# Attention scores in row groups of 64 queries and two heads over 192 keys, instead of 128 queries of one head over 256

## The chip, the cores and the metric

The kernel runs on one core of one Trainium2 chip. The metric is the device time of one launch in microseconds (us): 1665.48 us, the median of three runs (1665.45 to 1665.97). TensorE (PE) multiplies matrices, VectorE (DVE) and ScalarE (ACT) work elementwise, GpSimd (POOL) does small copies, clears and part of the DMA issues, SyncE (SP) issues the other DMAs. PEld is TensorE's weight load, which runs beside its matmuls. Each engine works through its own instructions in a fixed order and waits for the others at semaphores.

## The reference, cut to what matters

One layer of a hybrid decoder, in f32, for two request groups with shared weights: 1024 prompt tokens and 8 sample sequences of 8 tokens each (64 tokens), which makes T = 1088 columns. One input projection gives q (16 heads of 64), k and v (4 heads of 64), the two halves of a gated unit and two gates. Branch A is attention with a window of 128 and one learned sink per head:

```python
delta = i + WINDOW - j                       # query i of a block of 128, key j of 256: the block before and this one
band = (delta >= 0) & (delta < WINDOW)
s = einsum('bnqkgd,bnskd->bnkgqs', q, k) * HEAD_DIM ** -0.5
s = where(mask, s, NEG_INF)
p = softmax(concatenate([s, sink], -1))[..., :-1]
o = einsum('bnkgqs,bnskd->bnqkgd', p, v)
```

A query i can see only the keys i < j <= i + 128 of the 256. The sample tokens see their 128 cached keys and the new keys of their own sequence. Branch B is a gated unit, a causal depthwise convolution of width 31, LayerNorm, swish and a projection. Both branches are gated and added, and an output projection, a feed-forward part with a convolution of width 3, and the norms follow.

## The kernel before

**Numbers.** Most products are computed in three f32r matmuls of split operands (high by high, high by low, low by high; `mm3`, L190 to L192), for each of eight k tiles of 128 rows. Tokens go in three chunks of 384, 384 and 320 columns.

**Stages.** Weight tiles stream in an order that is written out by hand (`SEQUENCE`): q, k, v, the gated unit's halves b and a, and the gates. When k and v of a half are there, the attention of half p = 0 (heads 0 to 7) and later of p = 1 runs between the k tiles of the other streams. After that come the output product of the attention (`phase_y`, which reloads half 0 of the attention output from DRAM, L935 and L936), LayerNorm, the output projection, the feed-forward part, and the tail.

**The attention units.** `plan_units(p)` makes a list of steps for eight blocks of 128 queries and four sample units, each with a due time counted in k tiles. `tick()` is called at each k tile and issues the steps that are due. A block has two halves g. For each half there is one `scores` step (due 0 and 5), `turn` steps (due 14 and 19; one each for the keys of the block before and of this one) and a `mix` step (due 20 and 25). Blocks follow each other after 22 k tiles in half 0 and 19 in half 1.

- `scores`: four heads, each two matmuls (L396, L397) with 128 queries of one head as the weights and 256 keys as columns (128 keys in block 0), into PSUM banks "aux".
- `softmax`: GpSimd copies the four sinks into the fifth column group of the tile p (L362). VectorE scales, masks and takes the row minimum in one operation for each head (L368, the reduce). ScalarE takes exponentials with the sum (L373), VectorE the reciprocal (L375), ScalarE normalises (L377).
- `turn`: four transposes (L406), then the result is split into a high part by ScalarE (L225, pth) and a low part by VectorE (L226, ptl).
- `mix`: products with v (L418, L419), copied and added into the tile av (L424, L425). At the second half the result is split back into the q tiles, which so become the attention's output. Half 0 is written to DRAM by GpSimd (`attn_spill`, L443, L444).
- `sample_unit`: two f32 matmuls against the cached keys kp and two against the new keys ks (L459), a softmax with one reduce for each of the two, two transposes and the mix.

**The convolution of branch B** (`conv`) runs on VectorE alone, as 44 multiply-adds of 512 or 513 columns (L520) for each of eight channel tiles. Nothing in the attention reads it. Its place in VectorE's order is not written out: it is issued with a lower priority,

```python
with self.later(CONV_LATER):   # CONV_LATER = 1200: this many instructions later in the order of priorities
    self.conv(i, u)
```

and the scheduler that builds the kernel puts each of its operations, by its own estimate of times, where VectorE has nothing of higher priority that is ready. The order so found is fixed in the built kernel.

**Layouts.** q is a tile of [128, 4, 1088]: two heads of 64 dimensions on the partitions (one half g live, the other the low part), four head pairs, the tokens. `masks` holds 640 columns: the band of 256, the cached keys' 128, four times 64 new keys. The tile p is [128, 4, 260], a new one for each `scores` step out of two buffers.

Of the kernel before, what the change touches and what calls it, by code (L numbers as in the profile page):

```python
# [6 lines left out]
F32 = mybir.dt.float32  # L7
# [110 lines left out]
MTOT = 2 * WIN + WIN + 4 * NS  # L118


class Build:
# [237 lines left out]
    def softmax(self, parts, pt, lo, width, nsink):  # L359
        nc = self.nc  # L360
        n = len(parts)
        nc.gpsimd.tensor_copy(pt[:, :, width:width + 1], nsink[:, :, None])  # L362
        nm = self.t(self.at, [P, 4], "nm", bufs=4)
        den = self.t(self.at, [P, 4], "den", bufs=4)
        for j in range(n):
            least = nsink[:, j:j + 1]
            for o, s, mask in parts[j]:
                nc.vector.tensor_tensor_reduce(  # L368
                    out=pt[:, j, o:o + s.shape[1]], in0=s, in1=mask, scale=-(HD ** -0.5), scalar=least,
                    op0=ALU.add, op1=ALU.min, accum_out=nm[:, j:j + 1])  # L370
                least = nm[:, j:j + 1]
        for j in range(n):
            nc.scalar.activation(pt[:, j, lo:width + 1], pt[:, j, lo:width + 1], AF.Exp, bias=nm[:, j:j + 1],  # L373
                                 scale=-1.0, accum_out=den[:, j:j + 1])
        nc.vector.reciprocal(den[:, :n], den[:, :n])  # L375
        for j in range(n):
            nc.scalar.activation(pt[:, j, lo:width], pt[:, j, lo:width], AF.Identity, scale=den[:, j:j + 1])  # L377

    def attn_unit(self, p, blk, st):
        nc = self.nc  # L380
        q, kd, kl = st["q"], st["kd"], st["kl"]
        qs = slice(blk * P, (blk + 1) * P)
        lo = WIN if blk == 0 else 0
        keys = slice((blk - 1) * P + lo, (blk + 1) * P + lo)
        mask = self.masks[:, lo:2 * WIN]
# [3 lines left out]
        def scores(g):  # L389
            pt = live[g]["pt"] = self.t(self.at, [P, 4, 2 * WIN + 4], "p", bufs=2)  # L390
            s = []
            for jj in range(2):
                ps = self.bank("aux").rearrange("p (a b) -> p a b", a=2)
                for j in range(2):
                    h = 2 * jj + j
                    nc.tensor.matmul(ps[:, j, :], q[g][:, h, qs], kd[g][:, keys], start=True, stop=False)  # L396
                    nc.tensor.matmul(ps[:, j, :], q[g][:, h, qs], kl[g][:, keys], start=False, stop=True)  # L397
                    s.append([(lo, ps[:, j, :2 * WIN - lo], mask)])
            hd = 4 * (2 * p + g)
            self.softmax(s, pt, lo, 2 * WIN, self.nsink[:, hd:hd + 4])  # L400

        def turn(g, kb):
            pt = live[g]["pt"]
            ps = self.bank("aux")
            for h in range(4):
                nc.tensor.transpose(ps[:, h * P:(h + 1) * P], pt[:, h, kb * P:(kb + 1) * P], self.ident)  # L406
# [5 lines left out]
        def mix(g):  # L412
# [27 lines left out]
    def attn_spill(self, st, cols):  # L440
        nc = self.nc
        for j in range(4):
            nc.gpsimd.dma_start(self.d_ah[j, :, cols], st["q"][0][:, j, cols].bitcast(F32))  # L443
            nc.gpsimd.dma_start(self.d_al[j, :, cols], st["q"][1][:, j, cols].bitcast(F32))  # L444

    def sample_unit(self, p, bp, st):
# [4 lines left out]
        def scores():  # L451
            kp = self.t(self.at, [P, 2, WIN], "kp", bufs=1)
            vp = live["vp"] = self.t(self.at, [P, 2, P], "vp", bufs=1)
            nc.gpsimd.dma_start(kp, self.a["kpT"][p, :, 2 * bp:2 * bp + 2, :])
            nc.gpsimd.dma_start(vp, self.a["vp"][2 * bp:2 * bp + 2, :, p * P:(p + 1) * P].rearrange("b k d -> k b d"))
            ps = self.bank("aux")
            for d, x in ((slice(0, WIN), lambda b: kp[:, b, :]), (slice(WIN, 192), lambda b: k)):
                for b in range(2):
                    nc.tensor.matmul(ps[:, d], q[:, bp, b * HD:b * HD + P], x(b), start=b == 0, stop=b == 1)  # L459
# [14 lines left out]
        def mix():  # L474
# [7 lines left out]
            cs = slice(SEQ + 2 * bp * NT, SEQ + 2 * bp * NT + 2 * NT)  # L482
            for g in range(2):
                r = slice(g * HD, (g + 1) * HD)
                src = ov[r, g]
                dh = st["q"][0][r, :, cs].rearrange("p j (b t) -> p j b t", b=2)
                dl = st["q"][1][r, :, cs].rearrange("p j (b t) -> p j b t", b=2)
                self.split_ps(dh, dl, src)
            if p == 0 and bp == 3:
                self.attn_spill(st, slice(SEQ, T))  # L490
# [106 lines left out]
    def run(self):  # L597
        nc, tc, a = self.nc, self.tc, self.a
        es = ExitStack()
        with es:  # L600
            dp = es.enter_context(tc.tile_pool(name="dram", bufs=1, space=bass.MemoryType.DRAM))
            self.d_ah = self.t(dp, [4, P, T], "d_ah")
# [1075 lines left out]
```

## Time and profile before

| | |
|---|---|
| median of three runs | 1665.48 us (1665.45 to 1665.97) |
| span of the profiled execution | 1662.4 us |
| outside the span, against that median | 3.1 us |
| TensorE busy | 1652.5 us (99%) |
| VectorE busy | 1337.3 us (80%) |
| ScalarE busy | 866.3 us (52%) |
| GpSimd busy | 290.2 us (17%) |
| granted TensorE clock | nine tenths or more in every slice |

Rows of the profile name a line of the code, an engine, an operation and its tiles (out<-in). In a timeline the first number is the start and the second the duration, in microseconds from the start of the span. In a table of stretches the columns are named in its first line, and (x) is the number of instructions.

### The profile page before, as it was taken

How to read it: one execution, taken by the hardware profiler on the slowest of the kernel's cores; microseconds unless marked ns; L12 is line 12 of the kernel's file. 1: busy time of each engine (PE TensorE's matmuls, PEld its weight loads, DVE VectorE, ACT ScalarE, POOL GpSimd, SP SyncE). 2: the span in 40 equal slices, each digit the busy share in tenths (PEclk: the TensorE clock that was granted, in tenths of full speed). 3: DMA queues.
4: the chain of work that ended last, by engine and by line, in shares of the span. 5: the costliest groups of instructions: out<-in, count | busy, mean ns of one | idle time of the engine just before them, and what ended most of it. 6: DMA issues, size and time to landing. Idle time of an engine off the chain costs nothing.

```text
span 1662.4 us, 29877 instructions
## 1 busy us (share of the span) xinstructions
PE 1652.5 (99%) x11550; PEld 1636.9 (98%) x11550; DVE 1337.3 (80%) x2432; ACT 866.3 (52%) x1781; POOL 290.2 (17%) x483
## 2 busy tenths in 40 slices
PE   9999999999999999999999999999999999999998
PEld 9999999999999999999999999999999999999997
DVE  7899979999989986855545896777887786988867
ACT  6424368774488845973233454444444454524222
POOL 0100112231011111110000171344444320000000
PEclk9999999999999999999999999999999999999999
DMA  6221212232121265544343332244444324766403
GB/s 208 84 71 42 75 60 81 99 103 86 55 53 48 77 227 168 178 154 145 106 155 108 80 125 103 97 113 115 112 114 111 94 103 134 243 168 168 118 14 108
DMA packets 98623, 187.09 MB, mean 113 GB/s; under 512 B 22848, under 2 KB 57680, under 8 KB 98464
## 3 DMA queue, kind: packets, MB, share of 16 engines
q1 hardware_dynamic: 79152, 125.18, 24.3%
q0 software_dynamic: 18896, 59.72, 11.9%
q8 instruction: 91, 1.49, 0.4%
q14 instruction: 52, 0.43, 0.1%
q10 hardware_dynamic: 432, 0.27, 0.1%
HBM read 129.75 MB, written 57.35 MB: 113 GB/s over the span
## 4 chain that ended last, share of the span: by engine, by line
PE 91%; DVE 5%; ACT 2%; DMA 1%; issue 1%; ACTq 0%; DVEq 0%; SPq 0%
PE mm L190 23%; PE mm L192 23%; PE mm L191 23%; PE aux L190 6%; PE aux L192 6%; PE aux L191 6%; PE aux L406 1%; DVE c L520 1%; PE aux L418 1%; PE aux L419 1%; PE aux L396 1%; PE aux L397 1%; DVE bt L520 1%; DVE q L739 1%; DMA bw<-d_b 0%
## 5 line engine op out<-in xcount | busy, mean ns | idle before, releaser
L190 PE MATMUL mm<-xh,whi 128*128 128x384 f32 (+1 forms) x904 | 301.1, 333 | 0.0
L191 PE MATMUL mm<-xl,whi 128*128 128x384 f32 (+1 forms) x904 | 295.4, 327 | 0.1
L192 PE MATMUL mm<-xh,wlo 128*128 128x384 f32 (+1 forms) x904 | 295.4, 327 | 0.0
L191 PEld LDWEIGHTS mm<-xl,whi 128*128 128x128 f32 x904 | 170.0, 188 | 1.6 <-DVE xl L277 0.7
L190 PEld LDWEIGHTS mm<-xh,whi 128*128 128x128 f32 x904 | 169.8, 188 | 0.7
L192 PEld LDWEIGHTS mm<-xh,wlo 128*128 128x128 f32 x904 | 169.7, 188 | 0.1
L190 PE MATMUL mm<-mh,whi 128*128 128x272 f32 (+4 forms) x428 | 125.9, 294 | 0.0
L191 PE MATMUL mm<-ml,whi 128*128 128x272 f32 (+4 forms) x428 | 125.1, 292 | 0.0
L192 PE MATMUL mm<-mh,wlo 128*128 128x272 f32 (+4 forms) x420 | 123.5, 294 | 0.0
L1172 DVE SCALAR_TENSOR_TENSOR acc<-st,fc,acc 128x1104 f32<-128x1104 f32 x88 | 119.8, 1364 | 2.8 <-ACT acc L1170 2.0
L171 ACT CAST whi<-wraw 128x1024 fp32r<-128x1024 f32 (+1 forms) x76 | 74.2, 981 | 79.8 <-PE mm L191 59.7
L520 DVE SCALAR_TENSOR_TENSOR bt<-u,consts,bt 128x513 f32<-128x513 f32 x120 | 89.8, 748 | 0.7
L520 DVE SCALAR_TENSOR_TENSOR c<-sm,hsum,c 128x512 f32<-128x512 f32 x120 | 89.6, 747 | 0.7
L172 DVE TENSOR_TENSOR wlo<-wraw,whi 128x1024 fp32r<-128x1024 f32 (+1 forms) x76 | 86.1, 1136 | 4.9 <-ACT whi L171 4.6
L520 DVE SCALAR_TENSOR_TENSOR c<-u,consts,c 128x512 f32<-128x512 f32 x112 | 83.7, 747 | 0.5
L190 PEld LDWEIGHTS mm<-mh,whi 128*128 128x128 f32 x428 | 80.5, 188 | 0.2
L191 PEld LDWEIGHTS mm<-ml,whi 128*128 128x128 f32 x428 | 80.6, 188 | 0.0
L192 PEld LDWEIGHTS mm<-mh,wlo 128*128 128x128 f32 x420 | 79.0, 188 | 0.0
L1152 POOL COPY st<-co 128x16 f32<-128x16 f32 x44 | 75.6, 1724 | 0.2 <-issue 0.2
L191 PE MATMUL mm<-tl,whi 128*128 128x272 f32 x240 | 69.6, 290 | 0.0
L1320 ACT COPY st<-mm 128x272 f32<-128x272 f32 (+2 forms) x133 | 44.6, 349 | 47.8 <-PE mm L192 47.8
L192 PE MATMUL mm<-th,whi 128*128 128x272 f32 x240 | 69.3, 289 | 0.0
(462 smaller groups left out, 5491.6 us busy)
## 6 DMA issues: line engine op xcount, KB each, us to landing
wraw<-wall SPq DMA_DIRECT2D x118, 512.0 KB, 3.8
bw<-d_b SPq DMA_DIRECT2D x42, 272.0 KB, 3.4
d_b<-gd POOLq DMA_DIRECT2D x36, 272.0 KB, 6.1
d_b<-acc POOLq DMA_DIRECT2D x24, 272.0 KB, 3.3
ar<-wdn SPq DMA_DIRECT2D x32, 192.0 KB, 4.3
d_g<-acc POOLq DMA_DIRECT2D x10, 544.0 KB, 4.3
ga<-d_ga SPq DMA_DIRECT2D x8, 544.0 KB, 4.0
gb<-d_gb SPq DMA_DIRECT2D x8, 544.0 KB, 3.6
```

The lines of the kernel that those rows point to most:

```text
L171: self.cast = self.nc.scalar.copy(h[:, z], r[:, z]).ins
L172: self.nc.vector.tensor_tensor(l[:, z], r[:, z], h[:, z].bitcast(F32), ALU.subtract)
L190: mm(ps, wh, xh, start=first, stop=False, skip_group_check=more)
L191: mm(ps, wh, xl, start=False, stop=False, skip_group_check=more)
L192: mm(ps, wl, xh, start=False, stop=last, skip_group_check=more)
L396: nc.tensor.matmul(ps[:, j, :], q[g][:, h, qs], kd[g][:, keys], start=True, stop=False)
L397: nc.tensor.matmul(ps[:, j, :], q[g][:, h, qs], kl[g][:, keys], start=False, stop=True)
L406: nc.tensor.transpose(ps[:, h * P:(h + 1) * P], pt[:, h, kb * P:(kb + 1) * P], self.ident)
L520: mac = lambda o, x, w: nc.vector.scalar_tensor_tensor(o, x, w, o, ALU.mult, ALU.add)
L1152: nc.gpsimd.tensor_copy(ss[:, :, 0:2], co[:, f, 2:].rearrange("p (b t) -> p b t", b=NB))
L1172: nc.vector.scalar_tensor_tensor(acc, st[:, k:k + AW], fw(f, k), acc, ALU.mult, ALU.add)
L1320: op(d, r(ps))
```

## The change

Three things, in one edit.

**Row groups.** A `scores` step still makes four groups of 128 rows. A group now holds 64 queries (f = 0 or 1: the first or second half of the block) of two heads, and not 128 queries of one head. 64 queries can see 191 keys at most, so a group's columns are 192 keys (64 or 128 in block 0) in place of 256. To have 64 queries of two heads side by side, q is stored as [128, 17, 4, 64], in tiles of 64 tokens (`NQ`, `HQ`), and all that reads or writes it follows: `q_evac` writes with a stride, the spill is one DMA for each of two tiles, the reload and the output product in `phase_y` read runs of 64 tokens.

**The tile p.** There are two tiles for all steps (`p_start`), in which the columns that no query of a group sees are cleared once. The sink's column now lies beside the 192 keys, ahead of them for f = 0 and behind them for f = 1, and each group gets its own copy of one column by GpSimd, four for each step.

**Sample units.** GpSimd copies the new keys behind the cached ones, the scores of all 192 keys come from two f32 matmuls in one group, and one reduce takes them all. The masks grow to 960 columns.

The number of instructions changes so. TensorE: of 256 scores matmuls, 224 go from 256 to 192 columns, and of the 32 of block 0, which have 128, 16 keep them and 16 have 64. The sample scores go from 16 matmuls of 128 and 16 of 64 columns to 16 of 192. VectorE: 112 reduces go from 256 to 192 columns, eight from 128 to 64, and the sample's 16 become eight. GpSimd: 192 more sink copies, eight key copies, four clears. The multiply-adds of the convolution, their number and their priority offset are untouched.

```diff
--- before.py
+++ after.py
@@ -115,7 +115,11 @@
     COFF[_n] = (_o, _w)
     _o += _w
 CTOT = _o
-MTOT = 2 * WIN + WIN + 4 * NS
+HQ = P // 2
+HK = WIN + HQ
+PT = 2 * WIN + 8
+NQ = T // HQ
+MTOT = HK + NB // 2 * (WIN + NS)
 
 
 class Build:
@@ -356,54 +360,56 @@
         return self.consts[:, o + i:o + i + n]
 
 
-    def softmax(self, parts, pt, lo, width, nsink):
+    def softmax(self, rows):
         nc = self.nc
-        n = len(parts)
-        nc.gpsimd.tensor_copy(pt[:, :, width:width + 1], nsink[:, :, None])
+        n = len(rows)
         nm = self.t(self.at, [P, 4], "nm", bufs=4)
         den = self.t(self.at, [P, 4], "den", bufs=4)
-        for j in range(n):
-            least = nsink[:, j:j + 1]
-            for o, s, mask in parts[j]:
-                nc.vector.tensor_tensor_reduce(
-                    out=pt[:, j, o:o + s.shape[1]], in0=s, in1=mask, scale=-(HD ** -0.5), scalar=least,
-                    op0=ALU.add, op1=ALU.min, accum_out=nm[:, j:j + 1])
-                least = nm[:, j:j + 1]
-        for j in range(n):
-            nc.scalar.activation(pt[:, j, lo:width + 1], pt[:, j, lo:width + 1], AF.Exp, bias=nm[:, j:j + 1],
-                                 scale=-1.0, accum_out=den[:, j:j + 1])
+        for j, (s, mask, least, out, _) in enumerate(rows):
+            nc.vector.tensor_tensor_reduce(
+                out=out, in0=s, in1=mask, scale=-(HD ** -0.5), scalar=least,
+                op0=ALU.add, op1=ALU.min, accum_out=nm[:, j:j + 1])
+        for j, (*_, ext) in enumerate(rows):
+            nc.scalar.activation(ext, ext, AF.Exp, bias=nm[:, j:j + 1], scale=-1.0, accum_out=den[:, j:j + 1])
         nc.vector.reciprocal(den[:, :n], den[:, :n])
-        for j in range(n):
-            nc.scalar.activation(pt[:, j, lo:width], pt[:, j, lo:width], AF.Identity, scale=den[:, j:j + 1])
+        for j, (*_, out, _) in enumerate(rows):
+            nc.scalar.activation(out, out, AF.Identity, scale=den[:, j:j + 1])
 
     def attn_unit(self, p, blk, st):
         nc = self.nc
         q, kd, kl = st["q"], st["kd"], st["kl"]
-        qs = slice(blk * P, (blk + 1) * P)
-        lo = WIN if blk == 0 else 0
-        keys = slice((blk - 1) * P + lo, (blk + 1) * P + lo)
-        mask = self.masks[:, lo:2 * WIN]
         kbs = (1,) if blk == 0 else (0, 1)
         live = [{}, {}]
 
         def scores(g):
-            pt = live[g]["pt"] = self.t(self.at, [P, 4, 2 * WIN + 4], "p", bufs=2)
-            s = []
-            for jj in range(2):
+            pt = self.p_tiles[self.p_next % 2]
+            self.p_next += 1
+            live[g]["pt"] = pt.rearrange("p (s c) -> p s c", s=4)
+            first = 2 * (2 * p + g)
+            least = self.nsink[:, first:first + 2]
+            rows = []
+            for f in range(2):
+                lo = WIN if blk == 0 else f * HQ
+                n = (f + 3) * HQ - lo
+                keys = slice((blk - 1) * P + lo, (blk - 1) * P + lo + n)
                 ps = self.bank("aux").rearrange("p (a b) -> p a b", a=2)
-                for j in range(2):
-                    h = 2 * jj + j
-                    nc.tensor.matmul(ps[:, j, :], q[g][:, h, qs], kd[g][:, keys], start=True, stop=False)
-                    nc.tensor.matmul(ps[:, j, :], q[g][:, h, qs], kl[g][:, keys], start=False, stop=True)
-                    s.append([(lo, ps[:, j, :2 * WIN - lo], mask)])
-            hd = 4 * (2 * p + g)
-            self.softmax(s, pt, lo, 2 * WIN, self.nsink[:, hd:hd + 4])
+                for jj in range(2):
+                    qj = q[g][:, 2 * blk + f, 2 * jj:2 * jj + 2, :].rearrange("p h i -> p (h i)")
+                    nc.tensor.matmul(ps[:, jj, :n], qj, kd[g][:, keys], start=True, stop=False)
+                    nc.tensor.matmul(ps[:, jj, :n], qj, kl[g][:, keys], start=False, stop=True)
+                    at = (2 * f + jj) * PT + 4 + lo
+                    e = at - 1 + f
+                    sink = at + n if f else at - 1
+                    nc.gpsimd.tensor_copy(pt[:, sink:sink + 1], least[:, jj:jj + 1])
+                    rows.append((ps[:, jj, :n], self.masks[:, HK - n:HK], least[:, jj:jj + 1],
+                                 pt[:, at:at + n], pt[:, e:e + n + 1]))
+            self.softmax(rows)
 
         def turn(g, kb):
             pt = live[g]["pt"]
             ps = self.bank("aux")
             for h in range(4):
-                nc.tensor.transpose(ps[:, h * P:(h + 1) * P], pt[:, h, kb * P:(kb + 1) * P], self.ident)
+                nc.tensor.transpose(ps[:, h * P:(h + 1) * P], pt[:, h, 4 + kb * P:4 + (kb + 1) * P], self.ident)
             ph = self.t(self.at, [P, 512], "pth", F32R, bufs=2)
             pl = self.t(self.at, [P, 512], "ptl", F32R, bufs=2)
             self.split_ps(ph, pl, ps)
@@ -418,16 +424,15 @@
                 nc.tensor.matmul(av, v, ph, start=kb == kbs[0], stop=False)
                 nc.tensor.matmul(av, v, pl, start=False, stop=kb == kbs[-1])
             if g == 0:
-                live[0]["t"] = self.t(self.at, [P, 4 * P], "av").rearrange("p (a b) -> p a b", a=4)
+                live[0]["t"] = self.t(self.at, [P, 4 * P], "av")
             t = live[0]["t"]
-            av = av.rearrange("p (a b) -> p a b", a=4)
             nc.scalar.copy(t[r], av[o])
             nc.vector.tensor_tensor(t[r], av[r], t[r], ALU.add)
             if g == 1:
-                self.split_ps(q[0][:, :, qs], q[1][:, :, qs], t)
+                here = lambda x: x[:, 2 * blk:2 * blk + 2].rearrange("p f h i -> p (f h i)")
+                self.split_ps(here(q[0]), here(q[1]), t)
             if p == 0 and g == 1 and blk in (3, 7):
-                b0 = (blk - 3) * P
-                self.attn_spill(st, slice(b0, b0 + 4 * P))
+                self.attn_spill(st, 2 * blk - 6, 2 * blk + 2)
 
         steps = []
         for g in range(2):
@@ -437,11 +442,9 @@
             steps.append((A_MIX[g], lambda g=g: mix(g)))
         return steps
 
-    def attn_spill(self, st, cols):
-        nc = self.nc
-        for j in range(4):
-            nc.gpsimd.dma_start(self.d_ah[j, :, cols], st["q"][0][:, j, cols].bitcast(F32))
-            nc.gpsimd.dma_start(self.d_al[j, :, cols], st["q"][1][:, j, cols].bitcast(F32))
+    def attn_spill(self, st, a, b):
+        for d, q in ((self.d_ah, st["q"][0]), (self.d_al, st["q"][1])):
+            self.nc.gpsimd.dma_start(d[:, a:b], q[:, a:b].bitcast(F32))
 
     def sample_unit(self, p, bp, st):
         nc = self.nc
@@ -449,25 +452,26 @@
         live = {}
 
         def scores():
-            kp = self.t(self.at, [P, 2, WIN], "kp", bufs=1)
+            kp = self.t(self.at, [P, 2, WIN + NS], "kp", bufs=1)
             vp = live["vp"] = self.t(self.at, [P, 2, P], "vp", bufs=1)
-            nc.gpsimd.dma_start(kp, self.a["kpT"][p, :, 2 * bp:2 * bp + 2, :])
+            nc.gpsimd.dma_start(kp[:, :, 0:WIN], self.a["kpT"][p, :, 2 * bp:2 * bp + 2, :])
+            nc.gpsimd.tensor_copy(kp[:, :, WIN:], k[:, None, :].to_broadcast([P, 2, NS]))
             nc.gpsimd.dma_start(vp, self.a["vp"][2 * bp:2 * bp + 2, :, p * P:(p + 1) * P].rearrange("b k d -> k b d"))
-            ps = self.bank("aux")
-            for d, x in ((slice(0, WIN), lambda b: kp[:, b, :]), (slice(WIN, 192), lambda b: k)):
-                for b in range(2):
-                    nc.tensor.matmul(ps[:, d], q[:, bp, b * HD:b * HD + P], x(b), start=b == 0, stop=b == 1)
-            pt = live["pt"] = self.t(self.at, [P, 1, 196], "sp", bufs=1)
-            mo = 2 * WIN
-            mn = mo + WIN + NS * bp
-            self.softmax([[(0, ps[:, 0:WIN], self.masks[:, mo:mo + WIN]),
-                           (WIN, ps[:, WIN:192], self.masks[:, mn:mn + NS])]], pt, 0, 192, self.nsrow[:, p:p + 1])
+            n = WIN + NS
+            ps = self.bank("aux")[:, :n]
+            for b in range(2):
+                nc.tensor.matmul(ps, q[:, bp, b * HD:b * HD + P], kp[:, b, :], start=b == 0, stop=b == 1)
+            pt = live["pt"] = self.t(self.at, [P, n + 4], "sp", bufs=1)
+            least = self.nsrow[:, p:p + 1]
+            nc.gpsimd.tensor_copy(pt[:, n:n + 1], least)
+            mask = self.masks[:, HK + n * bp:HK + n * (bp + 1)]
+            self.softmax([(ps, mask, least, pt[:, 0:n], pt[:, 0:n + 1])])
 
         def turn():
             pt = live["pt"]
             tr = self.bank("aux")
-            nc.tensor.transpose(tr[:, 0:P], pt[:, 0, 0:P], self.ident)
-            nc.tensor.transpose(tr[:, P:2 * P], pt[:, 0, 64:192], self.ident)
+            nc.tensor.transpose(tr[:, 0:P], pt[:, 0:P], self.ident)
+            nc.tensor.transpose(tr[:, P:2 * P], pt[:, NS:NS + P], self.ident)
             ts = live["ts"] = self.t(self.at, [P, 4 * P], "av")[:, 0:2 * P]
             nc.scalar.copy(ts, tr[:, 0:2 * P])
 
...
@@ -632,7 +636,9 @@
 
     def derive(self):
         nc = self.nc
-        nc.vector.tensor_scalar(self.nsink, self.c("sink", 0, 16), -1.0, None, ALU.mult)
+        for x in range(2):
+            r = slice(x * HQ, (x + 1) * HQ)
+            nc.vector.tensor_scalar(self.nsink[r], self.c("sink", 0, 16)[r, x::2], -1.0, None, ALU.mult)
         nc.vector.tensor_scalar(self.cb2, self.c("cb", 0, KT), 2.0, None, ALU.mult)
         w = self.c("cw", 0, KT * CW).rearrange("p (i k) -> p i k", i=KT)
         hv = self.hsum.rearrange("p (i k) -> p i k", i=KT)
...
@@ -734,9 +740,10 @@
                 m = min(n, SEQ - o)
                 for g in range(2):
                     r, x = [slice(y * HD, (y + 1) * HD) for y in (g, 1 - g)]
-                    q = st["q"][g][:, j, o:o + m]
-                    nc.scalar.copy(q[r], ps[r, :m])
-                    nc.vector.tensor_tensor(q[x], ps[r, :m], q[r].bitcast(F32), ALU.subtract)
+                    q = st["q"][g][:, o // HQ:(o + m) // HQ, j, :]
+                    src = ps[r, :m].rearrange("p (b i) -> p b i", i=HQ)
+                    nc.scalar.copy(q[r], src)
+                    nc.vector.tensor_tensor(q[x], src, q[r].bitcast(F32), ALU.subtract)
                 if m < n:
                     for g in range(2):
                         r = slice(g * HD, (g + 1) * HD)
@@ -795,6 +802,14 @@
                     nc.scalar.copy(self.vs[64:128, :], ps[64:128, :256])
                     nc.gpsimd.dma_start(a["o_vn"], self.vs[64:128, :])
 
+        def p_start():
+            self.p_next = 0
+            self.p_tiles = [self.t(self.at, [P, 4 * PT], f"p{x}", bufs=1) for x in range(2)]
+            for t in self.p_tiles:
+                t = t.rearrange("p (s c) -> p s c", s=4)
+                nc.gpsimd.memset(t[:, 0:2, 4 + HK:4 + 2 * WIN], 0.0)
+                nc.gpsimd.memset(t[:, 2:4, 4:4 + HQ], 0.0)
+
         def plan_units(p):
             st = states[p]
             todo = [("u", b) for b in range(NBLK)]
...
@@ -929,11 +944,12 @@
                 a0_es = ExitStack()
                 a0 = pool(a0_es, "a0")
                 self.lt = pool(a0_es, "lt")
-                ah = self.t(a0, [P, 4, T], "ah", F32R)
-                al = self.t(a0, [P, 4, T], "al", F32R)
-                for (o, w) in CHUNKS:
-                    nc.sync.dma_start(ah[:, :, o:o + w].bitcast(F32), self.d_ah[:, :, o:o + w].rearrange("j p t -> p j t"))
-                    nc.sync.dma_start(al[:, :, o:o + w].bitcast(F32), self.d_al[:, :, o:o + w].rearrange("j p t -> p j t"))
+                ah = self.t(a0, [P, NQ, 4, HQ], "ah", F32R)
+                al = self.t(a0, [P, NQ, 4, HQ], "al", F32R)
+                for o, w in CHUNKS:
+                    b = slice(o // HQ, (o + w) // HQ)
+                    nc.sync.dma_start(ah[:, b].bitcast(F32), self.d_ah[:, b])
+                    nc.sync.dma_start(al[:, b].bitcast(F32), self.d_al[:, b])
             if kind == "b":
                 u = do_b(i)
             elif kind == "a":
...
@@ -965,7 +982,8 @@
         def xa(c, k):
             o, n = CHUNKS[c]
             h, l = (ah, al) if k < 4 else (bh, bl)
-            return h[:, k % 4, o:o + n], l[:, k % 4, o:o + n]
+            b = slice(o // HQ, (o + n) // HQ)
+            return h[:, b, k % 4, :], l[:, b, k % 4, :]
 
         def do_o(m):
             t = self.t(self.lt, [P, T], "ga", bufs=2)
...
```

More of the change, by code (lines that the diff above doesn't have):

```diff
@@ L724, in q_tiles @@
             if "q" not in st:
-                st["q"] = [self.t(qp, [P, 4, T], f"q{g}", F32R) for g in range(2)]
+                st["q"] = [self.t(qp, [P, NQ, 4, HQ], f"q{g}", F32R) for g in range(2)]
                 st["qs"] = self.t(qp, [P, NB // 2, 3 * 8 * NT], "qs")
@@ L812, in phase_x @@
         p0 = pool(p0_es, "p0", "left")
-        spare = [q[:, 3, :DM] for q in q_tiles(0)["q"]]
+        spare = [q[:, :NQ - 1].rearrange("p b h i -> p (b h i)")[:, 3 * DM:] for q in q_tiles(0)["q"]]
         self.slot = lambda i: (None, spare) if i == 4 else (p0, "xy"[i - 2]) if 2 <= i < FIRST else (self.wp, i % 2)
@@ L1590, in pack_masks @@
     n = np.arange(NS)[None]
-    new = [(n // NT == (2 * bp + b)[:, None]) & (n % NT <= t[:, None]) for bp in range(4)]
-    ok = np.concatenate([band, past] + new, 1)
+    sample = []
+    for bp in range(NB // 2):
+        sample += [past, (n // NT == (2 * bp + b)[:, None]) & (n % NT <= t[:, None])]
+    ok = np.concatenate([band] + sample, 1)
     return np.where(ok, 0.0, -1e30).astype(np.float32)
```

22 lines of the change are left out of this document (12 added, 10 removed).

## The prediction

> **What bounds the kernel now.** I read the page first: busy time by engine, the span in slices, and the chain that ended last.
>
> ```profile
> span 1662.4 us, 29877 instructions
> PE 1652.5 (99%) x11550; PEld 1636.9 (98%) x11550; DVE 1337.3 (80%) x2432; ACT 866.3 (52%) x1781; POOL 290.2 (17%) x483
> DVE  7899979999989986855545896777887786988867
> ...
> PE 91%; DVE 5%; ACT 2%; DMA 1%; issue 1%; ACTq 0%; DVEq 0%; SPq 0%
> ```
>
> TensorE is busy for 99% of the span. It has about 10 us left in which other work could hide, and whatever makes it wait is added to the time. But VectorE is no spare engine: each slice is 41.6 us, and from the 7th to the 14th (249 to 582 us), where the attention of both half passes runs, VectorE stands at nine tenths in all but one. Next, TensorE's own waits:
>
> ```profile
> PE mm L629 <- DVE warm L622: 1.1, 1, 1.1
> PE mm L190 <- DVE H L1456: 0.9, 1, 0.9
> PE aux L418 <- ACT pth L225: 0.8, 1, 0.8
> ```
>
> The longest wait inside the attention is 0.8 us. So today softmax and turn keep up, and the question is by how much. The busy time of each engine in two stretches answers that. The first runs from the first reduce of the 6th group of scores to that of the 16th, the second from the 21st group's to the 32nd's (there are 32: two half passes p, eight blocks, two halves g). The same stretches are shown again for the convolution's multiply-adds alone (L520, "macs").
>
> ```profile
> core 0: us, PE busy (x) PEld busy (x) DVE busy (x) ACT busy (x) POOL busy (x), PEclk, DMA share, GB/s
> 251.40:350.10 98.70, 98.70 (x642) 96.13 (x641) 96.38 (x217) 78.81 (x200) 21.78 (x43) 1.00 0.28 90
> 484.00:578.80 94.80, 94.74 (x620) 91.65 (x619) 92.10 (x218) 78.50 (x205) 15.36 (x31) 1.00 0.20 65
> ```
> ```profile
> 251.40:350.10 98.70, 36.39 (x51) 1.00 0.28 90
> 484.00:578.80 94.80, 35.47 (x50) 1.00 0.20 65
> ```
>
> VectorE is idle for 2.3 us of 98.7 and for 2.7 of 94.8. It is as full as TensorE, and more than a third of its time goes to 51 and 50 macs which belong to the convolution and not to the attention. None of TensorE's longest waits is for a mac's result, but VectorE works in a fixed order, so every mac that stands ahead of a reduce delays that reduce.
>
> **The change on VectorE: the order.** The instructions of the two built kernels can be counted in VectorE's own order. Ahead of the first reduce of the 6th, 9th, 11th, 13th and 16th group stand 132, 151, 162, 176 and 183 macs now, and 132, 160, 176, 191 and 214 in the changed kernel. Ahead of the 21st, 25th, 29th and 32nd: 264, 288, 308 and 314 now, 265, 301, 328 and 348 after. The differences between stretch ends, 183-132 and 314-264, are the 51 and 50 macs that the trace shows, so the count is the one that ran. After the change the stretches hold 82 and 83: 31 and 33 more. They are not new work; they are drawn forward from later, where VectorE has room, into stretches where it has none. The price of a mac, and of the reduces that get narrower:
>
> ```profile
> 604.42 0.75 DVE L520 SCALAR_TENSOR_TENSOR c<-sm,hsum,c 128x512 f32<-128x512 f32 x1
> 605.08 0.75 DVE L520 SCALAR_TENSOR_TENSOR bt<-u,consts,bt 128x513 f32<-128x513 f32 x1
> ...
> 460.37 0.48 DVE L368 CUSTOM_DVE_ANT_0 p<-aux,masks,nsink 128x256 f32<-128x256 f32 x1
> ...
> 461.18 0.48 DVE L368 CUSTOM_DVE_ANT_0 p<-aux,masks,nsink 128x256 f32<-128x256 f32 x1
> ...
> 450.70 0.35 DVE L368 CUSTOM_DVE_ANT_0 p<-aux,masks,nsink 128x128 f32<-128x128 f32 x1
> ...
> 451.25 0.34 DVE L368 CUSTOM_DVE_ANT_0 p<-aux,masks,nsink 128x128 f32<-128x128 f32 x1
> ...
> 321.09 0.35 DVE L368 CUSTOM_DVE_ANT_0 sp<-aux,masks,nsrow 128x128 f32<-128x128 f32 x1
> 321.37 0.75 DVE L520 SCALAR_TENSOR_TENSOR c<-u,consts,c 128x512 f32<-128x512 f32 x1
> 322.03 0.28 DVE L368 CUSTOM_DVE_ANT_0 sp<-aux,masks,nm 128x64 f32<-128x64 f32 x1
> 322.23 0.09 DVE L368 DVE_READ_ACCUMULATOR2_ANT nm<- 128x1 f32 x1
> ```
>
> Neighbours overlap a little, so I price by the step from start to start: a mac 0.66 us (604.42 to 605.08), a reduce of 256 keys 0.405 (460.37 to 461.18, two steps), of 128 keys 0.275 (450.70 to 451.25, two steps). No 192-key reduce is in the trace; it lies between, and by the middle it costs 0.34. So each narrowed reduce saves 0.065 (bounds 0 and 0.13). A sample unit's two reduces cost 0.28 and 0.20 now (321.09 to 321.37, 322.03 to 322.23), one of 192 will cost 0.34: 0.14 less, some three units in a stretch.
>
> First stretch: 31 x 0.66 = +20.5; 40 reduces x 0.065 = -2.6; sample -0.4: VectorE's work ahead of the 16th group grows by 17.5 us. Second: 33 x 0.66 = +21.8; 44 x 0.065 = -2.9; -0.4: 18.5 us. Together 36.0.
>
> How much of that does TensorE not notice? Two covers: VectorE's idle time, 2.3 + 2.7 = 5.0 us, and the distance from the softmax's end to the transposes that read it.
>
> ```profile
> 353.89 1.71 ACT L377 ACTIVATE p<-p,den 128x256 f32<-128x256 f32 x4
> ...
> 357.85 0.60 PE L406 MATMUL aux<-consts,p 128*128 128x128 f32 x4
> ```
>
> This group's last normalisation ends at 353.89 + 1.71 = 355.60 and TensorE takes the transposes at 357.85: 2.25 us of margin. Behind that TensorE waits in order, and the projection matmuls behind the transposes wait with it. With the margin alone, once a stretch, 36.0 - 4.5 = 31.5 is left; with the idle time too, 26.5; with neither, 36.0. I take 31.5: the idle time is mostly VectorE waiting for ScalarE or TensorE inside the softmax chain (reduce, exponential, reciprocal, normalise), and such waits come back whenever TensorE stands. The stall isn't returned later. After the 16th group VectorE has fewer macs left, but TensorE is 99% busy there and can't run ahead.
>
> **The change on TensorE.** Rows for the width of a matmul, by steps again:
>
> ```profile
> 303.62 0.28 PE L396 MATMUL aux<-kd,q 128*128 128x256 f32 x1
> ...
> 304.56 0.34 PE L190 MATMUL mm<-xh,whi 128*128 128x384 f32 x1
> ...
> 46.11 0.28 PE L334 MATMUL aux<-identr,rowsh 80*128 80x80 f32 x1
> ...
> 46.45 0.28 PE L334 MATMUL aux<-identr,rowsl 80*128 80x80 f32 x1
> ...
> 320.05 0.60 PE L459 MATMUL aux<-kp,qs 128*128 128x128 f32 x4
> 320.49 0.56 PE L459 MATMUL aux<-ks,qs 128*128 128x64 f32 x4
> 320.86 0.39 PE L190 MATMUL mm<-xh,whi 128*128 128x320 f32 x1
> ...
> 1650.29 0.39 PE L190 MATMUL mm<-mh,mh 128*128 128x512 f32 x1
> ...
> 1650.99 0.59 PE L1509 MATMUL aux<-fssq,mean 128*128 128x256 f32 x2
> ```
>
> Eight scores matmuls of 256 keys take 304.56 - 303.62 = 0.94, that is 0.1175 each; 80 columns still take (46.45 - 46.11) / 3 = 0.113. So 224 matmuls cut to 192 keys save some 0.004 each, 1 us in all: below the width of 256 the columns no longer set the step. The Trainium skill says two things of this. "TensorE: Matmul & The Clock Gate", section "Back-to-back issue gap", gives about 81 ns at 128 columns and 131 at 512 for sustained streams, by which an estimate for 192 is 89 ns and the saving would be 6 us. The same page's section "LDWEIGHTS (loading the stationary operand)" gives 107 ns for 128 weight columns whatever is multiplied. The 113 ns at 80 columns agrees with the second and not with the first.
>
> The sample scores take 320.86 - 320.05 = 0.81 us per unit: four instructions at 0.11 and four at 0.093. One group of four at 0.11 (as for 128 keys) to 0.165 (in proportion to the keys) takes 0.44 to 0.66. Eight units save 1.2 to 3.0; I take 2. Both savings, 3 us, lie nearly all in stretches where VectorE now sets the pace and shorten only TensorE's wait there: zero in the sum.
>
> The output product reads its tokens in runs of 64 now. Three matmuls of 512 take 1650.99 - 1650.29 = 0.70, 0.233 each, two of 256 0.235: a matmul's fixed part is some 0.002. 576 matmuls in 4.7 more runs each would cost 0.002 x 2700 = 5 us if a run cost that; no row shows a cost per run at all, and I take 0.
>
> **Other engines.** ScalarE's narrower exponentials and normalisations come from an engine that is idle for 20 of 98.7 us: nothing. The q evacuations in runs of 64, the masks, the four clears and eight key copies on GpSimd (22 of 98.7 us busy) and the fewer, larger spills: nothing. On SyncE's queue two loads of the convolution's result now stand ahead of the attention's reload; they'd hold that up only if the convolution ended late, and it ends earlier. GpSimd's sink copies go from one of four columns to four of one column:
>
> ```profile
> L362 POOL COPY p<-nsink x32: 186/192/2291, 203.6 to 575.9; 128x4 f32<-128x4 f32 x32
> ```
> ```profile
> 356.05 2.29 POOL L362 COPY p<-nsink 128x4 f32<-128x4 f32 x1 [1.37 <-PE aux L406]
> ```
>
> At the median, four take 0.77 us instead of 0.19, beside the four reduces (1.36 us): nothing. At the longest, four would take 9 us, with the exponentials behind them.
>
> **Sum.** 1662.4 + 31.5 = 1693.9 us of span. The profiled execution is 3.1 us shorter by its span than the median of the runs, 1665.5, and I add that: 1697.
>
> **Rivals.**
> *VectorE's lag stays covered.* Then only TensorE's savings count: 1665.5 less 1 for the scores and 1.2 to 3.0 for the samples, 1661.5 to 1663.3, faster. It needs a margin of over 17.5 us in each stretch; the rows show 2.25 and idle times of 2.3 and 2.7. Chance 0.05.
> *GpSimd's copies lag.* One copy of four columns took 2.29 us while macs ran back to back on VectorE, and the median is 0.19. With more macs in the stretches each of the four copies can be caught. At 1.2 us each a group's exponentials start 4.8 - 1.4 = 3.4 us later, some 1.2 beyond the margin of 2.25, and in a quarter to half of the 22 groups in the stretches (my choice, since the median copy is a short one) that is +7 to +13, 1704 to 1710. It decides from 0.9 us a copy (3.6 = 1.36 + 2.25). The Trainium skill, "SBUF — State Buffer", section "SBUF: two separate sides", describes an exclusive lock between a VectorE operation with two SBUF inputs and a GpSimd operation that reads SBUF; the spread from 186 to 2291 ns agrees. Chance 0.07.
> *Narrow matmuls run at the sample's rate per column.* At 0.165 instead of 0.1175, 224 cost +10.6; the 22 of 32 groups inside the stretches hide it behind VectorE, the rest costs 3: 1700; hidden nowhere, 1708. The 80-column row speaks against it. Chance 0.05.
> *The lag is absorbed in good part*, because the macs ahead leave gaps at other places of the softmax chain: 1666 to 1684. Chance 0.04.
>
> **Numbers.** The main case has 0.79, with its own range of 1690 to 1702 (26.5, less 2 for TensorE's savings outside the stretches, to 36.0). The range reaches below to 1684 (26.5 less 3 for TensorE's savings, and 5 for a second such margin in each stretch) and above to 1711 for the copies. A measurement here can tell 0.2% (3.3 us) from no change. Faster than that only by the first rival, which lies on both sides of the limit: 0.04; within it that rival's rest and the lower end of the last one, 0.02; slower 0.94.
>
> **What would show it.** Right: 82 and 83 macs between the same groups' first reduces; TensorE waiting at the transposes, the mixes and the scores for VectorE or ScalarE, some 15 us in the first stretch and 16 in the second, growing from about the 9th and the 25th group on; VectorE at 97% and more there; scores steps near 0.113. Wrong: those macs there, and no waits of TensorE; or waits that the copies on GpSimd release; or scores steps of 0.16; or time lost after the attention, in the output product.

## The result and the profile after

The changed kernel takes 1701.47 us (median of five runs, 1699.27 to 1703.24) against 1665.97 for the kernel before in the same series. The ratio is 1.0217, 95% interval 1.0205 to 1.0230: slower by 2.2%. The forecast was 1697, range 1684 to 1711. The page's span, busy time, VectorE's slices and the chain's shares by engine:

```profile
span 1697.5 us, 29932 instructions
PE 1663.3 (98%) x11518; PEld 1638.4 (97%) x11518; DVE 1328.6 (78%) x2417; ACT 857.6 (51%) x1781; POOL 321.0 (19%) x573
DVE  7999969996959982875554897778888786988867
...
PE 80%; DVE 16%; ACT 2%; issue 1%; DMA 1%; ACTq 0%; DVEq 0%
```

VectorE does 8.7 us less work in all than before (1328.6 against 1337.3), and yet its share of the chain that ended last went from 5% to 16%. TensorE's waits:

```profile
PE aux L425 <- DVE ptl L230: 9.1, 11, 1.7
PE aux L398 <- DVE ptl L230: 6.6, 6, 2.4
PE aux L424 <- DVE nm L369: 3.7, 1, 3.7
PE aux L412 <- DVE nm L369: 2.6, 2, 1.9
PE aux L424 <- ACT pth L229: 2.2, 3, 1.0
```

The longest wait in the attention was 0.8 us before; now these rows hold 23 waits, at the mix (L424, L425), at the scores (L398, which wait for a PSUM bank) and at the transposes (L412), and nearly all are for VectorE. Now the same two stretches (6th to 16th and 21st to 32nd group, first reduce to first reduce), all work and then the macs alone (L524):

```profile
252.87:367.35 114.48, 105.34 (x652) 97.99 (x651) 113.29 (x244) 75.55 (x197) 36.74 (x68) 1.00 0.26 77
505.27:615.45 110.18, 100.65 (x607) 93.31 (x606) 109.24 (x246) 75.86 (x206) 26.08 (x62) 0.95 0.17 53
```
```profile
252.87:367.35 114.48, 57.68 (x82) 1.00 0.26 77
505.27:615.45 110.18, 59.03 (x83) 0.95 0.17 53
```

82 and 83 macs, as the built order said, and VectorE busy for 99% of both stretches. They grew from 98.70 to 114.48 us and from 94.80 to 110.18: +15.8 and +15.4, 31.2 together. The rest of the 35.1 us by which the span grew is mostly one place between the stretches, which the prediction did not have. Here it is on ScalarE, VectorE and TensorE, from three timelines; the numbers in brackets are idle time before the instruction and what ended it:

```profile
474.75 1.28 ACT L691 ACT_TABLE_LOAD   x1
476.05 1.21 ACT L691 ACTIVATE u<-u 128x1024 f32<-128x1024 f32 x2
477.27 1.28 ACT L373 ACT_TABLE_LOAD   x1
...
480.46 0.58 ACT L429 COPY av<-aux 64x512 f32<-64x512 f32 x1
```
```profile
480.47 0.18 DVE L374 RECIPROCAL den<-den 128x4 f32<-128x4 f32 x1 [3.51 <-ACT p L373]
481.08 0.68 DVE L430 TENSOR_TENSOR av<-aux,av 64x512 f32<-64x512 f32 x1 [0.43 <-ACT av L429]
481.69 0.40 DVE L369 CUSTOM_DVE_ANT_0 p<-aux,masks,nsink 128x192 f32<-128x192 f32 x1
```
```profile
478.40 0.27 PE L399 MATMUL aux<-kl,q 128*128 128x192 f32 x1
483.10 0.50 PE L424 MATMUL aux<-pth,v 128*128 128x512 f32 x1 [3.71 <-DVE nm L369]
```

The scores of the 20th group were done soon after 478.40, but their reduces (from 481.69) stand behind a reciprocal and an addition that wait for ScalarE, which is loading tables for a sigmoid and back. Until the reduces release the bank, the mix waits. Before, the same reduces (the first and the last of four) stood ahead of that reciprocal:

```profile
462.62 0.48 DVE L368 CUSTOM_DVE_ANT_0 p<-aux,masks,nsink 128x256 f32<-128x256 f32 x1 [0.96 <-PE aux L397]
...
463.84 0.48 DVE L368 CUSTOM_DVE_ANT_0 p<-aux,masks,nsink 128x256 f32<-128x256 f32 x1
...
465.47 0.18 DVE L375 RECIPROCAL den<-den 128x4 f32<-128x4 f32 x1 [0.28 <-ACT p L373]
```

TensorE's own order moved here too: between the last scores matmul of the 20th group and this mix stand four projection matmuls in the change, where there were 17, which take some 3 us. Comparing the starts of the same projection matmuls in both traces, TensorE is 16.3 us late after the first half pass, gets 4.4 us later here, and is 36 us late after the second.

TensorE's clock is one more thing that the prediction does not have. In both stretches before, the granted clock is 1.00. In the change it is half at three places of the attention, the first of them right behind this wait:

```profile
483.70:487.10 3.40, 3.40 (x12) 3.31 (x11) 1.41 (x4) 2.73 (x10) 0.60 (x4) 0.50 0.00 0
562.20:565.60 3.40, 3.05 (x10) 2.86 (x11) 3.40 (x9) 0.31 (x1) 0.00 (x0) 0.50 0.72 144
606.60:613.40 6.80, 6.12 (x20) 5.21 (x19) 6.80 (x18) 3.55 (x12) 0.00 (x0) 0.50 0.17 66
```

At the first place the projection matmuls start 0.32 us apart (486.18 to 486.50), and 0.17 us apart after it (487.50 to 487.67). By these rows 13.6 us pass at half the clock, so an upper estimate of what they cost is 6.8 us; where VectorE sets the pace it can be less, and no run separates it.

### The profile page after: what moved, and what is told of

The parts are those of the page before. It is cut to its first block, busy times and chain, and to the rows that moved or that the text cites. A ratio compares the mean times of both kernels' runs of the same rounds, so it can differ in the third digit from the quotient of the medians.

```text
span 1697.5 us, 29932 instructions
## 1 busy us (share of the span) xinstructions
PE 1663.3 (98%) x11518; PEld 1638.4 (97%) x11518; DVE 1328.6 (78%) x2417; ACT 857.6 (51%) x1781; POOL 321.0 (19%) x573
## 4 chain that ended last, share of the span: by engine, by line
PE 80%; DVE 16%; ACT 2%; issue 1%; DMA 1%; ACTq 0%; DVEq 0%
PE mm L194 20%; PE mm L195 20%; PE mm L196 20%; PE aux L195 6%; PE aux L196 6%; PE aux L194 6%; DVE c L524 5%; DVE bt L524 2%; DVE p L369 2%; DVE ptl L230 1%; DVE wlo L176 1%; DVE av L430 1%; DVE c L530 1%; DVE c L531 1%; DVE q L230 0%
## 5 line engine op out<-in xcount | busy, mean ns | idle before, releaser
L524 DVE SCALAR_TENSOR_TENSOR bt<-u,consts,bt 128x513 f32<-128x513 f32 x120 | 90.1, 751 | 0.7
L524 DVE SCALAR_TENSOR_TENSOR c<-sm,hsum,c 128x512 f32<-128x512 f32 x120 | 89.8, 748 | 0.6 <-ACT c L536 0.2
L524 DVE SCALAR_TENSOR_TENSOR c<-u,consts,c 128x512 f32<-128x512 f32 x112 | 83.8, 748 | 0.6
L373 ACT ACTIVATE p<-p,nm 128x193 f32<-128x193 f32 (+2 forms) x128 | 56.2, 441 | 41.4 <-DVE nm L369 40.8
```

The source lines that it names most:

```text
L373: nc.scalar.activation(ext, ext, AF.Exp, bias=nm[:, j:j + 1], scale=-1.0, accum_out=den[:, j:j + 1])
L524: mac = lambda o, x, w: nc.vector.scalar_tensor_tensor(o, x, w, o, ALU.mult, ALU.add)
```

## The experiments

The theory: the loss is the order in which the built kernel works, above all VectorE's. (TensorE's hardly differs: of the 60 first matmuls of the mixes, 57 stand behind as many projection matmuls as before.) The changed operations themselves cost nothing. The rival: it is in the changed operations (sink copies, narrow matmuls, runs of 64).

**1 and 2: the orders exchanged.** The change with the order of before, and the kernel before with the order of the change. Each is the kernel itself plus a list of issue-order edges, the same lines in both:

```diff
+    def pin(self):   # PINNED: for each engine the other kernel's order, in this kernel's instruction names
+        known = {i.name: i for i in self.nc.cur_bb.bb.instructions}
+        for names in PINNED.values():
+            names = [f"I-{n}" for n in names if f"I-{n}" in known]
+            for x, y in zip(names, names[1:]):
+                self.tc.add_manual_dep(known[y], x, mybir.DependencyInfo(
+                    mybir.DependencyClass.NoSync, mybir.DependencyReason.DATA), reason="pin")
...
+        self.pin()
         self.phase_y(right, a0_es, states, ah, al)
```

> The change with every operation unchanged, but TensorE, VectorE and ScalarE made to issue in the order that the kernel before has (as edges of issue order alone, up to the end of the attention). Theory (the loss is VectorE's order, the work itself saves 3 us): 51 and 50 macs between the same first reduces, no wait of TensorE in the attention over 1 us, 1661.5 to 1663.5 us. Rival (the loss lies in the changed operations: four sink copies on GpSimd, narrow matmuls, runs of 64): it stays near 1701 us.

Measured: 1659.54 us against 1665.56, ratio 0.9967 (0.9955 to 0.9978). Its page, its waits, and its two stretches (all work, then macs):

```profile
span 1657.1 us, 29929 instructions
...
PE 97%; DVE 1%; ACT 1%; DMA 1%; issue 0%; DVEq 0%; SPq 0%; ACTq 0%
```
```profile
PE mm L201 <- DVE H L1490: 1.2, 2, 0.7
PE mm L648 <- DVE warm L641: 1.1, 1, 1.1
PE aux L439 <- ACT pth L236: 0.7, 1, 0.7
```
```profile
251.15:348.99 97.84, 97.84 (x634) 95.38 (x634) 93.56 (x214) 74.40 (x199) 33.17 (x69) 1.00 0.29 90
481.71:574.55 92.84, 92.84 (x612) 90.66 (x611) 88.87 (x213) 74.59 (x205) 28.72 (x63) 1.00 0.23 66
```
```profile
251.15:348.99 97.84, 36.31 (x51) 1.00 0.29 90
481.71:574.55 92.84, 35.43 (x50) 1.00 0.23 66
```

Every operation of the change is in it, and the whole loss is gone. TensorE doesn't stand in the stretches, and VectorE has 4.3 and 4.0 us to spare there where before it had 2.3 and 2.7. This version beats both kernels, by more than was expected (1661.5 to 1663.5): TensorE gains 4.9 us over the attention, not 3, and about 0.8 us more behind it.

> The kernel before with every operation unchanged, but the three engines made to issue in the order of the changed kernel. Theory: 82 and 83 macs in the stretches, as slow as the change or slower, since the reduces still take 0.405 and not 0.34 us: 1701.5 + 84 x 0.065 = 1707, between 1700 and 1713 us. Rival (the changed operations): near 1665.5 us.

Measured: 1717.93 us, ratio 1.0317 (1.0303 to 1.0331). So the order alone, with no operation changed, costs 52 us: more than the change, since the reduces stay wide, and more than was expected. Its stretches:

```profile
254.96:375.57 120.61, 111.66 (x651) 102.53 (x650) 116.58 (x247) 79.62 (x197) 21.76 (x42) 0.94 0.25 72
516.15:631.79 115.64, 104.41 (x614) 97.47 (x614) 112.74 (x251) 80.32 (x206) 15.26 (x30) 0.93 0.16 51
```

VectorE's work is 3.3 and 3.5 us more than in the change, as priced, but it also stands for 4.0 and 2.9 us in place of 1.2 and 0.9. An order made for other durations may fit these worse; the granted clock of TensorE is also lower there, 0.94 and 0.93 against 1.00 and 0.95 in the change, and no run separates the two.

**3 and 4: what moves the order.** The scheduler places operations by its own estimates, so some estimate must have changed. The suspect is the width of the scores matmuls. Two kernels test it, both with reduces as narrow as in the change: one with scores matmuls of 256 columns, and one of 252.

```diff
-                keys = slice((blk - 1) * P + lo, (blk - 1) * P + lo + n)
+                low = WIN if blk == 0 else 0            # and for 252: low = 4 * f, where blk > 0
+                keys = slice((blk - 1) * P + low, (blk + 1) * P)     # and for 252 four keys less at f == 0
+                w = keys.stop - keys.start
...
-                    nc.tensor.matmul(ps[:, jj, :n], qj, kd[g][:, keys], start=True, stop=False)
+                    nc.tensor.matmul(ps[:, jj, :w], qj, kd[g][:, keys], start=True, stop=False)
...
+                    sc = ps[:, jj, lo - low:lo - low + n]      # what softmax reads, as in the change
```

> The change, but each scores matmul multiplies all 256 keys (128 in block 0) and softmax reads its 192 of them. The scheduler left to itself then puts 152, 164, 176 and 188 macs ahead of the 9th, 11th, 13th and 16th group, nearly the order of before. Theory: 1662 to 1667 us. Rival (sink copies, runs of 64): near 1701 us. Rival (a matmul of 192 columns is slow on the chip): also 1662 to 1667, but then the steps of the scores matmuls in the changed kernel would have to be over 0.2 us.

> As with 256 columns, but four keys fewer: 252 columns, of which softmax reads the same 192. Nothing is left out of the result. The built order has 163, 176, 198 and 220 macs ahead of the 9th, 11th, 13th and 16th group and 306, 332 and 352 ahead of the 25th, 29th and 32nd: 6 and 4 more than the change at the stretch ends. Theory: slower than the change by about 10 x 0.66 = 7 us and up to 15, 1706 to 1717 us, from 1.6% fewer columns. Rivals: narrow matmuls slow on the chip: at most the change's 1701; copies or runs of 64: 1701.

Measured: 1663.73 us with 256 columns (ratio 0.9991, 0.9982 to 0.9999) and 1717.89 us with 252 (1.0317, 1.0303 to 1.0332), just above what was expected. Macs in the stretches, first for 256 and then for 252 columns:

```profile
252.72:350.97 98.25, 39.51 (x56) 1.00 0.28 90
482.94:578.02 95.08, 39.29 (x55) 1.00 0.22 65
```
```profile
254.31:375.50 121.19, 61.90 (x88) 0.93 0.24 73
513.04:630.87 117.83, 61.47 (x87) 0.97 0.16 51
```

With 256 columns the macs are nearly those of before although the reduces are narrow, so it is not the reduces that move them. Four columns fewer and the kernel takes 54 us longer. On the chip the matmuls differ by next to nothing; the first and last matmul of a group with 256 columns, and the second and last of one with 252:

```profile
304.76 0.28 PE L400 MATMUL aux<-kd,q 128*128 128x256 f32 x1
...
305.59 0.27 PE L401 MATMUL aux<-kl,q 128*128 128x256 f32 x1
```
```profile
300.62 0.28 PE L403 MATMUL aux<-kl,q 128*128 128x252 f32 x1
...
301.31 0.27 PE L403 MATMUL aux<-kl,q 128*128 128x252 f32 x1
```

Seven steps of 0.119 and six of 0.115. So it isn't the chip but the planner that treats a f32r matmul of 252 columns as another thing than one of 256. It orders as if TensorE were slower there and left VectorE time for macs. That is a reading of the orders and not shown: what exactly its estimate is stays open. The counts of macs and these two times are the evidence.

**5: the sample part alone**, in the kernel before.

> The kernel before with the sample units' part of the change alone (new keys copied behind the cached ones, one group of two matmuls of 192 columns, one reduce). The scheduler keeps the order of before (151, 162, 176, 184 and 288, 308, 314 macs ahead of the same groups). Theory: TensorE's saving shows in full, 32 instructions at 0.129 us in place of 32 at 0.111 and 32 at 0.092 (sums 4.1 and 6.5 us in the traces of the change and of before): 1665.5 - 2.4 = 1663.1. Rival (the key copy on GpSimd or the one reduce delays the unit): 1665 to 1668.

Measured: 1665.09 us against 1665.48, ratio 0.9999 (0.9991 to 1.0008): no difference. The instructions did get cheaper: the starts of the sample scores add up to 4.1 us instead of 6.5. But the same projection matmuls, 0.6 us ahead of before by 362 us, lose 1.1 us between 435 and 461 us, where a group of transposes and a mix start late, and end the attention 0.2 us behind. The expectation took a saving on TensorE for a saving of time; only where the order fits, as in experiment 1, did it stay.

**6: the sink copies doubled**, in the kernel with 256 columns.

```diff
-                    nc.gpsimd.tensor_copy(pt[:, sink:sink + 1], least[:, jj:jj + 1])
+                    for _ in range(2):
+                        nc.gpsimd.tensor_copy(pt[:, sink:sink + 1], least[:, jj:jj + 1])
```

> The change with matmuls of 256 columns, in which each of the four sink copies of a scores step is made twice (256 copies of one column for each 128). The macs' order is that of the same kernel without doubling. Theory: the copies are off the path, 1663 to 1665 us against 1663.7. Rival (copies that VectorE's operations catch hold up the exponentials): 16 groups with one caught copy more at some 2 us, less 2.25 of margin each, 5 to 15 us more: 1669 to 1679.

Measured: 1667.32 us, ratio 1.0006 (0.9997 to 1.0015) against 0.9991 (0.9982 to 0.9999) undoubled: between the two expectations. In the traces TensorE is 1.4 us later at one place, between 208 and 233 us, where the attention begins and the copies queue among GpSimd's DMA issues, and level from there to the end of the attention. But the traced execution is the fastest of eleven (1664.34 us); by the ratios the doubling costs 2.5 us. So 128 more copies cost some 1.5 to 2.5 us, and the change's own can't be the 36.

**7: the macs alone kept back.** The change, with each mac behind the VectorE operation that it follows in the order of before (one edge for each mac), and all else free.

> The change, in which each mac of the convolution is kept behind the operation that stands ahead of it in VectorE's order of before; all other operations are left to the scheduler. The counts of macs are those of before. Theory as first put (the macs are the whole loss): 1660 to 1666 us. Theory as widened (the scheduler fills the same supposed gaps with what else is ready, and puts reduces behind waits for ScalarE): part of the loss stays, 1674 to 1692 us.

Measured: 1686.68 us, ratio 1.0128 (1.0114 to 1.0141). The counts of macs are those of before, yet 21 of the 36 us remain. The theory as first put falls: the macs are the most visible part, not the whole. Other operations of VectorE and ScalarE still stand elsewhere than before, and which of them cost the rest was not separated. One part is the place between the half passes, where TensorE gets 5.6 us later in this run. Over the whole run TensorE waits mostly for the split that the mix reads, at the mixes (L434, L435) and at scores that need a PSUM bank (L408):

```profile
PE aux L435 <- DVE ptl L233: 5.8, 6, 1.4
PE aux L408 <- DVE ptl L233: 5.7, 6, 2.5
PE aux L434 <- ACT pth L232: 5.3, 2, 4.3
```

**8: the order of before only from the 17th to the 21st group.**

> The change, with the three engines in the order of before only from ahead of the 17th to the 21st group of scores (the start of half pass 1); elsewhere the scheduler's own order. In the change TensorE loses 4.4 us there, behind a wait of 3.7 us for a reduce (18th and 19th group). Theory (that loss is the reduces of one group put behind a reciprocal and an addition that wait for ScalarE): it goes and little else changes, 1701.5 - 4.4 = 1697, between 1694 and 1699 us. Rival (it is ScalarE's table loads and sigmoids, which before has at the same place): 1701 us.

Measured: 1697.68 us, ratio 1.0192 (1.0176 to 1.0208), 3.8 us less than the change. The wait of 3.7 us is gone with ScalarE's table loads still there, as long as in the change:

```profile
476.93 1.28 ACT L706 ACT_TABLE_LOAD   x1
...
479.45 1.28 ACT L380 ACT_TABLE_LOAD   x1
```

So the cause was the order at this place and not the table loads. The run puts back the orders of three engines, the reduces ahead of the reciprocal and the 17 projection matmuls ahead of the mix alike; which of the two counts for more is not shown.

## Why the prediction was right

**The order.** 31 and 33 more macs in the stretches: measured as counted. The stretches grew by 31.2 us against the forecast 31.5, but that so close a fit came out is luck, since the working has two errors that cancel. VectorE's busy time grew by 113.29 - 96.38 = 16.9 and 109.24 - 92.10 = 17.1, where 17.5 and 18.5 had been summed; and its idle time, which the sum left out as coming back, shrank by 1.1 and 1.8 (2.3 to 1.2, 2.7 to 0.9). 16.9 + 17.1 - 2.9 = 31.1. The margin of 2.25 between normalisation and transposes is no cover in these lengths.

**The signs.** VectorE is busy for 99% of the stretches and the waits are where they were expected. But TensorE is idle for 114.48 - 105.34 = 9.1 and 110.18 - 100.65 = 9.5 us there, not some 15 and 16. By the starts of its projection matmuls it falls 13.0 and 16.4 us behind inside them: a wait counts only from the modelled end of the matmul before it (479.06 + 0.33 to 483.10 is the wait of 3.71), and in the second stretch TensorE also ran at half the clock for a while. The first losses over 1 us come at 265 and 518 us, about the 7th and the 23rd group, not the 9th and the 25th.

**What was missed**: the 4.4 us between the stretches. The prediction counted macs and looked at no other order, neither at the reduces behind a reciprocal nor at TensorE's mix; experiment 8 gives 3.8 of it back. With it the forecast would have been 1701.

**The reason given** was too narrow. The text treated the count of macs as the cause, and asked neither why the scheduler moved them nor what else it moved. Experiment 7 shows that putting the macs alone back recovers 15 us of the 36; experiments 3 and 4 show that one property of the matmuls moves all of it.

**The durations.** A reduce of 192 keys was put at 0.34, a scores matmul at 0.113 us:

```profile
475.53 0.41 DVE L369 CUSTOM_DVE_ANT_0 p<-aux,masks,nsink 128x192 f32<-128x192 f32 x1
...
476.54 0.41 DVE L369 CUSTOM_DVE_ANT_0 p<-aux,masks,nsink 128x192 f32<-128x192 f32 x1
```
```profile
473.33 0.27 PE L399 MATMUL aux<-kl,q 128*128 128x192 f32 x1
...
474.00 0.27 PE L399 MATMUL aux<-kl,q 128*128 128x192 f32 x1
```

Three steps of 0.337 and six of 0.112. The estimate of 0.089 from the Trainium skill ("TensorE: Matmul & The Clock Gate", section "Back-to-back issue gap") did not come; that page's section "LDWEIGHTS (loading the stationary operand)", with 107 ns for 128 weight columns, is what the trace agrees with. TensorE's saving had been put at 3 us, 1 for the scores and 2 for the samples. In experiment 1 it is 2.4 and 2.4: summed over all starts, the scores take 28.4 us instead of 30.8, the samples 4.1 instead of 6.5. The term for the scores was too small because a step inside a group stood for all, and the mean of all 256 was 0.1205.

**The rivals.** *Lag covered*: it was not, since VectorE's work grew by 16.9 and 17.1 us and the stretches by 15.8 and 15.4. *Absorbed in good part*: for the same reason no. *Copies*:

```profile
L403 POOL COPY p<-nsink x128: 175/186/2407, 204.0 to 601.5; 128x1 f32<-128x1 f32 x128
```

The longest of 128 took 2.4 us and the median 0.19, as before; none of TensorE's long waits is released by one, and experiment 6 bounds them. *Narrow matmuls slow*: no, 0.112; this rival had the right object and the wrong place, for it is the planner that counts them slow. *Runs of 64 in the output product* had been bounded at 5 us and taken at 0: TensorE's lateness goes from 35.9 to 36.3 us over that stage, so 0.3.

## What to carry to other kernels

Where a scheduler fixes the order of each engine, an edit has two effects: what its operations cost, and where everything else is put. Count, in the built order, what stands ahead of the operations that the critical engine waits for, for all the engines that feed it; here counting the macs gave the sign, and the size with some luck, while all the operations got cheaper or stayed. And when an order moves without a reason in the durations on the chip, look for the width or the shape at which the planner's estimate jumps: keeping the matmul at 256 columns takes away the loss of 36 us (ratio 0.9991 to before, so hardly a gain), and pinning the order turns it into a gain of 6 us.

## What the runs showed of the hardware

A f32r matmul with 128 weight columns has a step of 0.112 us at 192 columns, 0.115 at 252 and 0.119 at 256: no jump at 256. In most stretches where TensorE often waits, its granted clock is lower: 0.95 in the second stretch of the change, 0.94 and 0.93 in experiment 2, 0.93 and 0.97 with 252 columns; but 1.00 in the change's first stretch, which waits as much, and 1.00 wherever it doesn't wait. VectorE was the bound in these stretches, so what that costs by itself isn't separated. One thing stays open: over the feed-forward part, which is the same in all kernels, those with the new layout of q gain some 1.5 us on the kernel before, and those with the old layout (experiments 2 and 5) don't.
